# Down projections of three feed-forward blocks: weights stationary, or activations stationary with four pairs by seven products

## Chip, cores and metric

One Trainium2 chip, one core of it. The metric is the device time of one execution in microseconds; lower is better. A profiled execution gives a trace, from which the rows shown below are taken. TensorE is called PE, VectorE DVE, ScalarE ACT, GpSimd POOL; SP is the engine that issues the loads. Ldweights (PEld) puts a 128x128 tile, the stationary operand, into the PE array; a matmul then streams the columns of the moving operand past it.

## What is computed

Two decoder layers over 256 tokens of 1024 features, float32. Each layer is a half-weighted feed-forward block, attention, and another half-weighted feed-forward block:

```python
def swiglu(h, w_gate, w_up, w_down):
    return (jax.nn.silu(h @ w_gate) * (h @ w_up)) @ w_down

for layer in range(DEPTH):                      # 2
    h = h + 0.5 * swiglu(rmsnorm(h, ffn1_norm[layer]), ...)   # D_FF 2816
    hn = rmsnorm(h, mix_norm[layer])
    if layer == 0: h = h + mixer_a(hn, ...)     # own q, k, v
    else:          h = h + mixer_b(hn, ...)     # q from hn, shared k, v
    h = h + 0.5 * swiglu(rmsnorm(h, ffn2_norm[layer]), ...)
    if layer == 0: shared = shared_kv(h, kv_norm, kv_w, pos)
return rmsnorm(h, final_norm)
```

## The kernel before

The stream lives in `hT`, with features on partitions: eight blocks (`d`, or `k` where they are contracted) of 128 features by 256 tokens. The stages run in the order f10, mixer a, f20, f11, mixer b, f21; the name of a feed-forward block is `f`, which of its layer's two it is, and the layer.

*Products in two parts.* Every float32 operand is split into a high part (ACT copies it, rounded, into `wh`, or the first half of an `x`) and a low part (DVE subtracts the high one: `wl`, or the second half). A product is high x high + high x low + low x high. `products_t` (L190) holds weights stationary: `wh` against the 512 columns of an `x` block (high and low, 256 tokens each), then `wl` against the 256 high columns. `product` (L181) holds activations stationary, 128 tokens at a time, against three times 512 columns of weights.

*Feed-forward.* `ffn_blocks` (L354) makes the 22 blocks of 128 hidden features, two at a time, each with 8 + 8 matmuls for gate and for up; `close` joins the two halves of the accumulators, applies the norm's row, silu and the product, and splits the result. The three inner blocks then call `down_t` (L320): four passes over pairs of output blocks, each over all 22 hidden blocks with weights stationary; the sum goes straight into `hT` (L332), and `norm.block` (L218) makes the next norm's scaled block `x` and its square at once. Six of the eight output blocks are thus done before the last pass.

*The last one, f21,* calls `down_last` (L435) instead, with tokens on partitions. Its hidden blocks are taken in 11 pairs. Four of them (`FAST`: 2, 4, 6, 7) are computed as a 2x2 block product by seven block products in place of eight: `quarter_sums` (L342) forms sums of the activations during gate and up (the tiles `left`), `load` (L459) forms sums of the weights (DVE one addition, POOL two), `fast` (L476) issues the seven products into `m1`, `m5`, `m6`, `m7` and three of the four outputs `c11`, `c12`, `c21`, `c22`, and `collect` (L486) combines them after the last fast pair. Two pairs are held back to the end, so that the outputs close one by one.

*Norms.* `finish` (L234) turns the sum of squares (POOL adds, L232) into a column per token tile by a PE product, an addition on DVE and a power on POOL. A stage that follows can begin before it: the factor is applied when its first accumulators are evacuated.

*PSUM.* Eight banks: five for accumulators (`acc`) and three for transposes and small things (`trt`), each set taken in rotation.

*Mixers.* An `Agenda` (L257) puts small steps (rotation, transposes of queries and keys, scores, softmax, values) between projection products by planned delays. `projections` (L720) goes over segments of weights; for each, four blocks of token tile 0, four of tile 1, the other four of tile 0, of tile 1. `evacuate` (L698) follows a tile's last block.

The order of the instructions on each engine is made by a scheduler when the kernel is built; each engine then executes its own list strictly in order, waiting on semaphores. What is far apart in the code can stand close together there: the eight gains of the shared keys and values (`kx`, passed as `beside` to f11) stand within f20's down in the kernel before.

Of the kernel before, what the change touches and what calls it, by code (L numbers as in the profile page):

```python
# [15 lines left out]
P = 128  # L16
# [50 lines left out]
def trunk(ctx: ExitStack, tc: tile.TileContext, a: dict, out: bass.AP):  # L67
# [139 lines left out]
    def by_token(xs):  # L207

        return [[tuple(x[:, i, t * P:(t + 1) * P] for i in range(2)) for x in xs] for t in range(NT)]

    class Norm:

        def __init__(self, gi, name):
            self.gi, self.name, self.x, self.col, self.row = gi, name, [], None, None
# [103 lines left out]
    def down_t(name, w, blocks, norm):  # L320

        for p in range(KD // 2):
            acs = [acc(f"dn_{name}_{2 * p + b}") for b in range(2)]
            for k0 in range(0, KF, KD):
                k = min(KD, KF - k0)
                ws = unit(f"{name}_{p}_{k0}", k, S, [(None, rows(w, k0, k, p * S, S))])
                cut = [[tuple(v[:, b * P:(b + 1) * P] for v in pair) for pair in ws] for b in range(2)]
                products_t(acs, cut, blocks[k0:k0 + k], k0 == 0, k0 + k == KF)
            for b, ac in enumerate(acs):
                d = 2 * p + b  # L330
                for half in (ac[:, :S], ac[:, S:]):
                    nc.vector.scalar_tensor_tensor(hT[:, d, :], half, 0.5, hT[:, d, :], op0=ALU.mult, op1=ALU.add)  # L332
                norm.block(d)

# [19 lines left out]
    def ffn_blocks(name, wg, wu, norm, first=None, beside=(), sums=None):  # L354
# [42 lines left out]
        for f in range(0, KF, 2):  # L397
# [37 lines left out]
    def down_last(name, w, blocks, sums, h, weight, part, after, tail=2):  # L435
# [4 lines left out]
        c11, c12, c21, m1, m5 = [acc(f"dn_{name}_{n}") for n in ("11", "12", "21", "m1", "m5")]  # L440
        c22, m6, m7 = [trt(f"dn_{name}_{n}") for n in ("22", "m6", "m7")]
# [45 lines left out]

# [376 lines left out]
```

## Times and profile before

| what | value |
|---|---|
| three runs | 986.69, 986.85, 988.29 us; median 986.85 |
| profiled execution | 986.84 us, of which 985.1 is its span (first to last instruction) |
| granted PE clock | 0.999 |
| busy | PE 99%, weight loads 86%, DVE 76%, ACT 60%, POOL 22% |
| moved from memory | 173.99 MB at 178 GB/s |
| f_g, f_u matmuls (gate and up) | 688 of 512 columns and 688 of 256 columns each |
| dn_f matmuls (the three `down_t`) | 528 of 512 columns and 528 of 256 columns |

A row such as `L332 DVE ... gains_hT<-dn_f,gains_hT 128x256 ... x48 | 19.0, 417 | 23.1 <-PE dn_f L198` is a group: line, engine, operation, output and inputs, shape, count, then busy time in us, mean ns of one, idle time before it, and what ended the idle time. In the rows of the timeline the first two numbers are the start and the duration in us, and a bracket gives the idle time before and its releaser. Matmuls overlap, so the spacing of their starts says more than their durations. Numbers of tiles are left out in names: `wh_f_g` are the high parts of all gate weights, `x_n` the scaled blocks of all norms. The matmuls that a helper issues all carry the helper's line.

### The profile page before, as it was taken

The page shows a single profiled execution, that of the slowest core. Times are in us where ns is not written, and L with a number is a line of the kernel's source. Part 1 is how long each engine was busy: PE and PEld are TensorE (multiplying, and loading weights), DVE is VectorE, ACT ScalarE, POOL GpSimd, SP SyncE. Part 2 cuts the span into 40 slices and gives each one's busy share as a digit, 9 for nine tenths or more (in the row PEclk, how much of TensorE's full clock was granted, in tenths as well). Part 3 has the DMA queues.
Part 4 walks back from the last instruction along what each step waited for, and adds up shares of the span by engine and source line. Part 5 has one row for each costly group of instructions (what it writes and reads, how often), then busy time and mean ns, then how long its engine had stood idle before and what let it go on. Part 6 is the DMA issues. An engine that isn't in the chain of part 4 may idle for free.

```text
span 985.1 us, 15279 instructions
## 1 busy us (share of the span) xinstructions
PE 972.6 (99%) x5640; PEld 847.2 (86%) x5640; DVE 753.1 (76%) x1313; ACT 594.7 (60%) x1090; POOL 213.1 (22%) x220
## 2 busy tenths in 40 slices
PE   8999999999999999999999999999999999999997
PEld 5888888888889888888888888888888998888886
DVE  7987866677877788776668887657677778888996
ACT  7666654457776665654456556544577766666561
POOL 3211111122332211110112111111042422112461
PEclk9999999999999999999999999999999999999999
DMA  9876565655443556555655565665544255565351
GB/s 317 256 242 208 161 210 186 214 172 166 133 130 107 181 187 203 178 198 189 213 173 172 185 200 184 200 196 192 197 132 140 90 168 164 180 200 184 128 172 43
DMA packets 152251, 176.03 MB, mean 179 GB/s; under 512 B 3440, under 2 KB 140144, under 8 KB 152176
## 3 DMA queue, kind: packets, MB, share of 16 engines
q1 hardware_dynamic: 151328, 174.01, 55.1%
q8 instruction: 44, 0.72, 0.3%
q10 hardware_dynamic: 848, 1.05, 0.3%
q14 instruction: 31, 0.25, 0.1%
HBM read 173.99 MB, written 1.05 MB: 178 GB/s over the span
## 4 chain that ended last, share of the span: by engine, by line
PE 68%; ACT 2%; DVE 2%; issue 1%; POOL 0%; POOLq 0%; ACTq 0%; DVEq 0%
PE f_g L195 12%; PE f_u L195 12%; PE dn_f L195 8%; PE f_u L198 6%; PE f_g L198 6%; PE dn_f L198 4%; PE dn_f_d L184 1%; PE dn_f_d L186 1%; PE dn_f_d L188 1%; PE q_b L184 1%; PE kv_b L184 1%; PE q_b L188 1%; PE kv_b L188 1%; PE q_b L186 1%; PE kv_b L186 1%; PE ot_ao L546 1%
## 5 line engine op out<-in xcount | busy, mean ns | idle before, releaser
L195 PE MATMUL f_g<-x_n,wh_f_g 128*128 128x512 f32 x688 | 180.4, 394 | 0.0
L195 PE MATMUL f_u<-x_n,wh_f_u 128*128 128x512 f32 x688 | 177.3, 390 | 0.0
L371 POOL TENSOR_TENSOR j_f_u<-j_f_u,r_n 128x256 f32<-128x256 f32 x88 | 80.5, 917 | 376.2 <-DVE j_f_u L339 352.7
L195 PEld LDWEIGHTS f_u<-x_n,wh_f_u 128*128 128x128 f32 x688 | 129.2, 188 | 27.3
L195 PEld LDWEIGHTS f_g<-x_n,wh_f_g 128*128 128x128 f32 x688 | 124.0, 189 | 22.7
L195 PE MATMUL dn_f<-act_f,wh_f 128*128 128x512 f32 x528 | 126.5, 391 | 0.0
L159 DVE TENSOR_TENSOR wl_f_u<-raw_f_u,wh_f_u 128x1024 fp32r<-128x1024 f32 x86 | 118.5, 1380 | 2.9 <-ACT wh_f_u L158 2.8
L159 DVE TENSOR_TENSOR wl_f_g<-raw_f_g,wh_f_g 128x1024 fp32r<-128x1024 f32 x86 | 103.5, 1233 | 15.7 <-PE f_g L198 9.3
L195 PEld LDWEIGHTS dn_f<-act_f,wh_f 128*128 128x128 f32 x528 | 96.9, 188 | 18.6
L159 DVE TENSOR_TENSOR wl_f<-raw_f,wh_f 128x1024 fp32r<-128x1024 f32 x72 | 81.8, 1153 | 36.0 <-ACT wh_f L158 26.8
L198 PE MATMUL f_u<-x_n,wl_f_u 128*128 128x256 f32 x688 | 103.3, 283 | 0.0
L198 PE MATMUL f_g<-x_n,wl_f_g 128*128 128x256 f32 x688 | 102.7, 282 | 0.0
L198 PEld LDWEIGHTS f_g<-x_n,wl_f_g 128*128 128x128 f32 x688 | 96.4, 190 | 6.2
L158 ACT ACTIVATE wh_f<-raw_f 128x1024 fp32r<-128x1024 f32 x72 | 67.3, 978 | 49.5 <-PE dn_f L195 27.2
L158 ACT ACTIVATE wh_f_u<-raw_f_u 128x1024 fp32r<-128x1024 f32 x86 | 86.7, 1048 | 16.7 <-PE f_g L195 10.9
L158 ACT ACTIVATE wh_f_g<-raw_f_g 128x1024 fp32r<-128x1024 f32 x86 | 89.5, 1048 | 9.8 <-issue 6.0
L198 PEld LDWEIGHTS f_u<-x_n,wl_f_u 128*128 128x128 f32 x688 | 91.6, 192 | 0.0
L232 POOL TENSOR_TENSOR ss_n<-ss_n,sq_n 128x256 f32<-128x256 f32 x42 | 41.8, 996 | 221.6 <-ACT sq_n L231 220.7
L369 ACT ACTIVATE j_f_g<-j_f_g 128x256 f32<-128x256 f32 x88 | 36.7, 417 | 66.2 <-DVE j_f_g L368 65.8
L98 ACT ACTIVATE act_f<-j_f_g 128x256 fp32r<-128x256 f32 x80 | 33.0, 417 | 65.4 <-DVE j_f_g L379 65.3
L198 PEld LDWEIGHTS dn_f<-act_f,wl_f 128*128 128x128 f32 x528 | 68.1, 191 | 2.8
L198 PE MATMUL dn_f<-act_f,wl_f 128*128 128x256 f32 x528 | 69.0, 283 | 0.0
(553 smaller groups left out, 1795.8 us busy)
## 6 DMA issues: line engine op xcount, KB each, us to landing
raw_f_g<-in_ffn_w_gate_dram SPq DMA_DIRECT2D x43, 1024.0 KB, 5.4
raw_f_u<-in_ffn_w_up_dram SPq DMA_DIRECT2D x43, 1024.0 KB, 5.4
raw_f<-in_ffn_w_down_dram SPq DMA_DIRECT2D x24, 1024.0 KB, 5.2
raw_f_d<-in_ffn_w_down_dram SPq DMA_DIRECT2D x11, 1024.0 KB, 5.0
raw_f<-in_ffn_w_down_dram SPq DMA_DIRECT2D x12, 768.0 KB, 4.5
raw_qka<-in_a_w_qkv_dram SPq DMA_DIRECT2D x16, 512.0 KB, 4.3
raw_va<-in_a_w_qkv_dram SPq DMA_DIRECT2D x4, 1024.0 KB, 5.2
raw_ao<-in_a_w_o_dram SPq DMA_DIRECT2D x4, 1024.0 KB, 5.0
```

The lines of the kernel that those rows point to most:

```text
L98: nc.scalar.activation(hi, src, AF.Copy, scale=scale)
L158: nc.scalar.activation(wh, r, AF.Copy)
L159: nc.vector.tensor_sub(wl, r, wh.bitcast(F32))
L184: nc.tensor.matmul(ac, xh, wh, start=first, stop=False)
L186: nc.tensor.matmul(ac, xh, wl, start=False, stop=False)
L188: nc.tensor.matmul(ac, xl, wh, start=False, stop=last)
L195: nc.tensor.matmul(ac, wh, flat(x), start=first and i == 0, stop=False)
L198: nc.tensor.matmul(ac[:, :S], wl, x[:, 0, :], start=False, stop=last and i == len(ws) - 1)
L232: nc.gpsimd.tensor_tensor(self.ss, self.ss, sq, op=ALU.add)
L369: nc.scalar.activation(g, g, AF.Silu)
L371: nc.gpsimd.tensor_tensor(u, u, norm.row, op=ALU.mult)
L546: nc.tensor.matmul(ac, wl[:, d], hi, start=False, stop=k == KD - 1 and j == 1)
```

## The change

All four downs are now computed in the way of f21. The body of `down_last` becomes `quartered`, which returns a function `close` that finishes one output quarter (token tile `t`, feature half `c`). `down_last` uses it as before. The new `down` is used by f10, f20 and f11 in place of `down_t`:

- `collect` no longer adds to the stream; it returns four tiles (`co`), onto which the closed quarters are added (DVE, one operation each).
- The quarters close in the order (0,0), (1,0), (0,1), (1,1). `turn` transposes two feature blocks of both tiles into a `trt` bank (eight transposes for a half of 512 features, in two groups), adds them to `hT`, and norms the two blocks. The first half is turned ahead of the last block of quarter (0,1). The second half's two turns are put off (`norm.late`): a mixer's agenda takes them 1.5 and 2.0 after its start, a feed-forward block after its first contraction block.
- `x` is therefore looked up when it is used (`x[t](k)`), and in the mixers the column product of the norm and both evacuations of the first segment that needs it come after both token tiles.
- `left_sums` chooses where the quarter sums live. f10 and f20 have four homes, as f21 has; f11, in which the tiles of `kx` are in use, has three, and so three fast pairs (2, 4, 6) instead of four.
- Token tile 1's outputs `c21` and `c22` and the product `m6` now lie in the three transpose banks, `c11`, `c12`, `m1`, `m5`, `m7` in the accumulator banks.
- The gains `kx` now stand in f11's opening in ACT's and DVE's lists, not in f20's down.

```diff
@@ ffn_blocks, first two blocks
                             products_t([ac], [[(wh[:, cols], wl[:, cols])]], norm.x[k:k + 1], k == 0, k == KD - 1)
+                    while norm.late:
+                        norm.late.pop(0)()
@@
-    def ffn(name, layer, which, norm, after, first=None, beside=()):
+    def ffn(name, layer, which, norm, after, first=None, beside=(), homes=("kx4", "kx6", "qkh", "qkh")):
...
-        blocks = ffn_blocks(name, wg, wu, norm, first, beside)
+        sums = left_sums(homes)
+        blocks = ffn_blocks(name, wg, wu, norm, first, beside, sums)
...
-        down_t(name, wd, blocks, after)
+        down(f"{name}_d", wd, blocks, sums, after)
@@
-        c11, c12, c21, m1, m5 = [acc(f"dn_{name}_{n}") for n in ("11", "12", "21", "m1", "m5")]
-        c22, m6, m7 = [trt(f"dn_{name}_{n}") for n in ("22", "m6", "m7")]
+        c11, c12, m1, m5, m7 = [acc(f"dn_{name}_{n}") for n in ("11", "12", "m1", "m5", "m7")]
+        c21, m6, c22 = [trt(f"dn_{name}_{n}") for n in ("21", "m6", "22")]
@@
+        def close(t, c, cols=slice(0, 512), ac=None, between=None):
+            n = quarters[t][c][0] if ac is None else "end"
+            whole = quarters[t][c][1] if ac is None else ac
+            to = whole[:, :cols.stop - cols.start]
+            for j, (k, ws) in enumerate(held):
+                add(n, to, blocks[t][k], tuple(v[:, cols] for v in ws[c]), k == KF - 1)
+                if between is not None and j == len(held) - 2:
+                    between()
+            return whole
@@
+    def down(name, w, acts, sums, norm):
+        outs = []
+        close = quartered(name, w, acts, sums, 0.5, outs.extend)
+        def turn(c, half):
+            tr = trt(f"dt_{name}_{c}_{half}")
+            for i in range(2):
+                for t in range(NT):
+                    at = i * S + t * P
+                    nc.tensor.transpose(tr[:, at:at + P], outs[t][c][:, (2 * half + i) * P:(2 * half + i + 1) * P], ident)
+            d = 4 * c + 2 * half
+            h = hT[:, d:d + 2, :]
+            nc.vector.tensor_add(h, tr.rearrange("p (k s) -> p k s", s=S), h)
+            for i in range(2):
+                norm.block(d + i)
+        def turn_first():
+            for half in range(2):
+                turn(0, half)
+        for c in range(2):
+            for t in range(NT):
+                ac = close(t, c, between=turn_first if (t, c) == (0, 1) else None)
+                nc.vector.scalar_tensor_tensor(outs[t][c], ac, 0.5, outs[t][c], op0=ALU.mult, op1=ALU.add)
+        norm.late += [lambda half=half: turn(1, half) for half in range(2)]
@@ mixer
+        for norm in {id(norm): norm for norm, _, _ in segs}.values():
+            for i in range(len(norm.late)):
+                agenda.after(1.5 + 0.5 * i, lambda norm=norm: norm.late.pop(0)())
...
-                            product([acs[t]], *x[t][k], [w], k == 0, k == KD - 1)
+                            product([acs[t]], *x[t](k), [w], k == 0, k == KD - 1)
...
-                        if k0 + 4 == KD:
-                            if norm.col is None:
-                                norm.finish()
+                        if k0 + 4 == KD and norm.col is not None:
                             evacuate(i, t, norm.col[t], acs[t], parts)
+                if norm.col is None:
+                    norm.finish()
+                    for t in range(NT):
+                        evacuate(i, t, norm.col[t], acs[t], parts)
@@
-    ffn("f11", 1, 1, n3, n5, beside=[lambda k=k: kx.append(gain(k, 3, "kx", "kx")) for k in range(KD)])
+    ffn("f11", 1, 1, n3, n5, homes=("qkh", "qkh", "pT"), beside=[lambda k=k: kx.append(gain(k, 3, "kx", "kx")) for k in range(KD)])
```

More of the change, by code (lines that the diff above doesn't have):

```diff
@@ L317, in __getitem__ @@
             return self.parts[i]
[L320 to L333, printed above, removed]
     def joined(ac, name):
@@ L518, in down_last, with collected @@
+    def down_last(name, w, acts, sums, h, weight, part, after):
+        def collected(shared):
+            for t in range(NT):
+                for c in range(2):
+                    (nc.vector if t else nc.gpsimd).tensor_tensor(h[t][c], h[t][c], shared[t][c], op=ALU.add)
+        close = quartered(name, w, acts, sums, weight, collected)
         for t in range(NT):
             for c in range(2):
-                n, ac = quarters[t][c]
-                cut = 512 if (t, c) != (1, 1) else S
-                for k, ws in held:
-                    add(n, ac[:, :cut], blocks[t][k], tuple(v[:, :cut] for v in ws[c]), k == KF - 1)
+                n = 512 if (t, c) != (1, 1) else S
+                ac = close(t, c, slice(0, n))
```

46 lines of the change are left out of this document (24 added, 22 removed).

## Prediction

> **What bounds the kernel now.** I read the busy shares first, then what TensorE (PE) waits for, then single stages by windows.
>
> ```profile
> span 985.1 us, 15279 instructions
> PE 972.6 (99%) x5640; PEld 847.2 (86%) x5640; DVE 753.1 (76%) x1313; ACT 594.7 (60%) x1090; POOL 213.1 (22%) x220
> PEclk9999999999999999999999999999999999999999
> ...
> PE busy L118 <- DVE fill L115: 1.4, 1, 1.4
> PE f_g L195 <- ACT wh L173: 1.3, 2, 0.9
> PE po_b L637 <- DVE pT_b L94: 1.0, 1, 1.0
> ```
>
> PE is occupied 99% of the span at full clock, and its list of waits has six rows of 0.7 to 1.4 us, about 6 us in all. So time is won by issuing fewer PE columns and lost wherever PE begins to wait. The windows of the down stages (f10, f20, f11, f21 in the order of the program), and of f21's gate and up products, say what each costs (columns: length; PE, weight loads, DVE, ACT, POOL busy, each with its count; clock; DMA share; GB/s):
>
> ```profile
> 132.40:193.70 61.30, 61.30 (x355) 54.16 (x354) 38.46 (x51) 29.87 (x42) 7.40 (x6) 1.00 0.63 201
> 433.40:494.70 61.30, 61.30 (x355) 54.17 (x354) 40.84 (x56) 30.75 (x46) 7.71 (x6) 1.00 0.62 199
> 618.30:679.50 61.20, 61.20 (x354) 54.07 (x353) 38.46 (x49) 29.81 (x42) 7.76 (x6) 1.00 0.62 200
> 812.50:921.50 109.00, 109.00 (x639) 96.66 (x638) 90.70 (x158) 68.27 (x128) 22.05 (x22) 1.00 0.58 184
> 921.50:979.00 57.50, 57.46 (x266) 47.89 (x264) 50.23 (x54) 28.56 (x42) 28.60 (x13) 1.00 0.30 101
> ```
>
> The fifth row is the layout that the change gives to the other three: f21 already has act stationary and four pairs by seven products. PE never pauses there, nor in the stage before it (fourth row), where the quarter sums of the activations are formed. That is the best evidence in this case, because the copied work has been seen beside its own DVE, ACT and POOL load.
>
> **Part 1, the products.** Before, a down is 176 (block, output) pairs, each one 512-column and one 256-column matmul: 61.3/176 = 0.348 us. After, 7 ordinary pairs of 24 matmuls and 4 fast ones of 21 make 252 matmuls of 512 columns. f21 shows exactly that in 57.5 us, so 0.228 each; 12 of its matmuls are cut in two there, some 0.1 us. I take 57.4 for f10 and f20: **-3.9 us each**. f11 has homes for only three quarter sums, so 255 matmuls: 57.4 + 3 x 0.228 = 58.1, **-3.1 us**. Of the 3.9 about 2.7 is the four products left out (4 x 3 x 0.228) and 1.2 the orientation. SP issues 11 loads of 1024 KB per down for 12 smaller ones, the same 11 MB.
>
> **Part 2, the turns.** Each down adds 16 transposes of 128x128. The mixer's turn has the same form:
>
> ```profile
> 205.53 0.39 PE L188 MATMUL v_a<-wh_va,x_n 128*128 128x512 f32 x1
> 205.76 0.60 PE L692 MATMUL qt_a<-ident,rt_a 128*128 128x128 f32 x4
> 206.12 0.48 PE L184 MATMUL v_a<-wh_va,x_n 128*128 128x512 f32 x1
> 206.43 0.40 PE L186 MATMUL v_a<-wl_va,x_n 128*128 128x512 f32 x1
> ```
>
> Four take 0.36 us, and the next matmul takes 0.31 for 0.23, so two adjoining groups cost 0.36 + 0.36 + 0.08 = 0.8 us, and a down's two such places 1.6. **+4.8 us over three downs**, all on PE. Parts 1 and 2 together: -2.3, -2.3, -1.5, so **-6.1 us**.
>
> **Part 3, work that must stay hidden.** In gate and up, DVE gets the quarter sums and ACT their high halves; f21 hides the same. In the down, POOL adds eight half-blocks and DVE and ACT split seven pieces for four. One add was starved there:
>
> ```profile
> 934.30 11.38 POOL L468 TENSOR_TENSOR sum_f_d_6b<-sum_f_d_6ac,raw_f_d 128x512 f32<-128x512 f32 x1 [4.40 <-DVE sum_f_d_6ac L467]
> 948.61 1.56 DVE L455 TENSOR_TENSOR wl_f_d_6d<-sum_f_d_6d,wh_f_d_6d 128x512 fp32r<-128x512 f32 x1
> ```
>
> Pair 6 starts on PE after 138 matmuls, at 921.5 + 31.5 = 953.0, and first needs that last piece 15 matmuls later, at 956.4, while it is split by 950.2. The cover is 6 us; were it gone, PE would wait by the excess. I book zero.
>
> **Part 4, the hand-over to the next stage** is new, and its order shows in the built kernel. Let T be the end of the last product. Before, six of eight feature blocks were normed long before T. Now nothing of the stream is ready until both token tiles of a half are closed. The first turn (features 0 to 511) sits five products, 3.4 us, ahead of T; the second sits behind nine matmuls of the mixer (T+2.05), or behind the eight of f11's first block (T+1.4). Durations:
>
> ```profile
> 970.75 0.69 DVE L524 SCALAR_TENSOR_TENSOR h<-dn_f_d,h 128x512 f32<-128x512 f32 x1 [2.71 <-PE dn_f_d L188]
> 193.69 1.22 DVE L311 TENSOR_TENSOR wl_va<-raw_va,wh_va 128x1024 fp32r<-128x1024 f32 x1
> 922.40 2.31 DVE L455 TENSOR_TENSOR wl_f_d_2a<-raw_f_d,wh_f_d_2a 128x1024 fp32r<-128x1024 f32 x1
> L96 DVE SCALAR_TENSOR_TENSOR x_n<-gains_hT,x_n x48: 470/955/1049, 4.1 to 800.5; 128x256 fp32r<-128x256 f32 x48
> 195.28 0.51 ACT L98 ACTIVATE x_n<-gains_hT 128x256 fp32r<-128x256 f32 x1 [1.24 <-DVE gains_hT L332]
> 195.70 0.40 ACT L231 ACTIVATE sq_n<-gains_hT 128x256 f32<-128x256 f32 x1
> 192.03 2.01 ACT L309 ACTIVATE wh_va<-raw_va 128x1024 fp32r<-128x1024 f32 x2 [3.11 <-issue]
> 196.24 1.06 POOL L232 TENSOR_TENSOR ss_n<-ss_n,sq_n 128x256 f32<-128x256 f32 x1 [10.72 <-ACT sq_n L231]
> ```
>
> DVE, from T-3.6: two adds into hT (no row has the form; the 0.69 of the first row stands for it), low half of block 0, the closing sum of (tile 0, half 1), low halves 1 to 3, then the closing sum of (tile 1, half 1). ACT feeds it in steps of 0.4 to 0.5 and finishes high half 3 near T. A low half takes 0.47 alone and 0.96 beside a POOL add, and three POOL adds fall here. So block 3 is done at about T+1.5 and the last closing sum at T+2.2. The second turn waits for it: 0.8 us in f11, 0.15 in each mixer.
>
> *Mixer a, second half.* Behind the closing sum DVE has two weight splits (T+4.6), two adds (T+5.9), low half 4, a split of 1.22, then low halves 5 to 7. ACT has four weight copies until T+4.5. PE reaches block 4 at T + 24 x 0.228 + 0.8 + 0.15 = T+6.4 and wants low half 5 at T+7.5; DVE has it at T+8.0 to 8.4, or T+9.5 if the split takes the 2.31 of the third row. Between 0.4 and 2 us; I take 1.0, as most splits run near 1.22. The POOL sums end near T+10.5, before the column product at T+13.
>
> *f11, second half.* Blocks come 1.4 us apart, so low halves 4 to 7 are in time. But the eight shared-K/V gains, which f20's down used to hide, now stand on ACT in f11's opening, between a weight copy that waits for the last product of f11's first units and the copies that free the accumulators:
>
> ```profile
> 499.70 0.49 ACT L98 ACTIVATE x_kx<-gains_hT 128x256 fp32r<-128x256 f32 x1
> 506.00 0.50 PE L237 MATMUL col_n<-mean,ss_n 128*128 128x1 f32 x4
> 507.64 0.36 ACT L338 ACTIVATE j_f_g<-f_g 128x256 f32<-128x256 f32 x1
> 509.04 0.42 DVE L339 TENSOR_TENSOR j_f_g<-f_g,j_f_g 128x256 f32<-128x256 f32 x1
> 512.39 2.09 PE L195 MATMUL f_g<-x_n,wh_f_g 128*128 128x512 f32 x8
> ```
>
> Counted from the column product C: one copy to C+1.1, seven gains at 0.4 to C+3.9, two copies to C+5.9, the first accumulator copied and joined at C+6.8. PE wants its bank for the fourth block at C + (512.39 - 506.00) = C+6.4. A wait of 0.5 us, bounds 0 and 2.
>
> *Turn-in of queries.* The column product moved behind both token tiles, so both tiles' first turns now follow each other in each mixer:
>
> ```profile
> 202.65 0.71 POOL L241 TENSOR_TENSOR c_n<-v_n,expo 128x2 f32<-128x2 f32 x1 [2.99 <-DVE v_n L239]
> 203.39 0.69 ACT L703 ACTIVATE rt_a<-qk_a,c_n 128x512 f32<-128x512 f32 x1 [2.72 <-POOL c_n L241]
> 204.11 0.29 DVE L576 TENSOR_TENSOR ra_a<-rt_a,rot 128x128 f32<-128x128 f32 x1 [1.54 <-ACT rt_a L703]
> ```
>
> A split of 1.22 stands ahead of the small sum on DVE, then 0.71, two evacuations of 0.69 and eight rotations of 0.2 to 0.3: the second tile is ready near C+4.6, PE asks at C+4.2. **0.4 us in each mixer** (0 to 1).
>
> Waits together: mixer a 0.15 + 1.0 + 0.4, f11 0.8 + 0.5, mixer b 0.15 + 0.4, so **+3.4 us**, bounds 0 and 8. Where no wait comes, what hides it is the 5.5 to 6.4 us of PE work between a turn and the first use of its blocks.
>
> **The sum.** -6.1 + 3.4 = -2.7. The profiled execution took 986.84 us, 1.74 beyond its span, and the runs' median is 986.85; the same 1.74 stays. **984.1 us.**
>
> **Rivals.** (a) *All of Part 4 hides*, as f21's stage hides all of its own: 986.85 - 6.1 = 980.7. For it: the order was built with these chains in sight. Against it: the closing sum ends 0.8 behind PE's arrival in f11 by rows alone.
> (b) *The f11 opening costs more*: gains that f20's down hid become a wait, the join of the first accumulators late by the upper bound of 2 us, and DVE, held by a split behind the waiting copy, late with the row of norms too, another 0.5: 984.1 + 2.0 = 986.1, no change that can be told.
> (c) *Slower: DVE and POOL collide at the hand-over.* Each turn puts seven POOL adds among DVE's low halves and weight splits. If every one is slowed (eight low halves by 0.49, two splits by 1.09), DVE's chain is 6.1 us longer; 1.5 us of slack taken off, mixer a and f11 wait 4.6 more each and mixer b 1 more: 984.1 + 10.2 = 994.3, and with two thirds of it 990.9, which I take as its time. It decides from 4.7 us on (988.8). Against it: many splits of 1.2 us ran beside POOL adds as well.
> (d) *The products don't come denser*, PE waiting for the pieces of fast pairs: 1 us in each of the 11 gives 984.1 + 11 = 995. f21's row speaks against it.
>
> The Trainium skill, page "SBUF — State Buffer", section "Who interferes with whom", says that VectorE with two SBUF inputs and a GpSimd operation lock each other out for a whole instruction, and that issue order decides who waits. By it a low half would wait out a whole add, 1.06 us in place of my 0.49, and a turn with eight of them would be 4.6 us later still: an estimate that makes (c) the case. The trace agrees that they collide (0.47 against 0.96; the add of 11.38), but shows partial delays rather than a whole add for every operation.
>
> **Chances.** Sum as worked out (982.2 to 986) 0.52; (a) 0.20; (b) 0.14; (c) 0.11; (d) 0.03. The range 980.4 to 988.0 holds the first three and leaves out 14 in 100. Less than 0.2% (2 us) can't be told from no change here. Faster than 984.9: (a) and most of the first, 0.64; within 0.2%: the rest of the first and (b), 0.22; slower: 0.14.
>
> **What would show it.** The windows of the three downs: 57.4 + 0.8 us with PE full (Part 1 and first turn), f11's 58.1 + 0.8. Two groups of four transposes at 0.36 each. PE's waits: dt on DVE's closing sum of about 0.8 in f11 and under 0.3 in the mixers; qk_a's third matmul of blocks 5 to 7 on x_n; f_g of f11's fourth block on the join; qt on the rotations. If PE's list shows none of these, (a) holds; if gate and up stages or the fast pairs show waits, f21 was a bad guide and the sum falls.

## The result, and the profile after

The changed kernel took 984.54 us (median of 7 runs, 984.32 to 984.83) beside 986.91 us for the kernel before in the same comparison: a ratio of 0.9972, with a 95% interval of 0.996 to 0.9983. It is faster by 2.4 us; the prediction said 984.1. The profiled execution's span fell from 985.1 to 982.6 us. The head of the page after, and its list of what PE waited for:

```profile
span 982.6 us, 14865 instructions
PE 968.3 (99%) x5391; PEld 832.8 (85%) x5391; DVE 813.0 (83%) x1383; ACT 613.8 (62%) x1131; POOL 289.6 (29%) x242
...
PE qt_a L741 <- DVE rt_a L625: 1.7, 1, 1.7
PE busy L118 <- DVE fill L115: 1.4, 1, 1.4
PE qt_b L741 <- DVE rt_b L625: 1.0, 1, 1.0
```

PE executes 249 matmuls fewer. VectorE is busy 60 us more and GpSimd 77 us more, and yet the list has only two rows that are new: the query turns of the two mixers. The windows of the downs of f10, f11 and f21 (the first two up to their last product, so with their first turn; the second figure is PE's busy time):

```profile
132.40:190.50 58.10, 58.10 (x263) 48.20 (x262) 50.61 (x56) 34.08 (x50) 27.12 (x12) 1.00 0.61 211
...
616.10:674.90 58.80, 58.80 (x266) 48.74 (x265) 47.57 (x52) 32.40 (x47) 22.30 (x10) 1.00 0.60 207
918.90:976.40 57.50, 57.50 (x266) 47.94 (x264) 50.27 (x53) 28.52 (x42) 28.64 (x13) 1.00 0.29 101
```

PE is busy in all of 58.10 and 58.80 us: the new downs run as f21's always did, with one turn on top. To see where time went I read, in PE's timeline, when each stage's first product starts, and took the length of each stage (us):

| stage | before | after | difference |
|---|---|---|---|
| f10 down | 61.25 | 58.04 | -3.21 |
| mixer a (from its first product to f20's) | 116.20 | 119.57 | +3.37 |
| f20 down | 61.25 | 58.07 | -3.18 |
| f11 opening (to the column product) | 11.31 | 12.17 | +0.86 |
| f11, rest of gate and up | 112.26 | 112.25 | 0 |
| f11 down | 61.25 | 58.76 | -2.49 |
| mixer b | 116.66 | 118.78 | +2.12 |
| gate and up of f20 / f21 | 123.57 / 125.33 | 123.57 / 125.32 | 0 |

The stages add up to -2.5, the change of the span. Three downs give 8.9 us, and the stage behind each takes some back: 0.86 in f11, 2.1 in mixer b, 3.4 in mixer a. About 0.87 of each is the second turn itself. The rest is late starts: 2.5 us in mixer a and 1.25 in mixer b, of which PE's idle time in the timeline shows 1.7 and 1.1 (a product that waits also starts its follower some 0.1 us late, and very short waits leave no gap). Mixer a's hand-over in the timeline of after, first PE and ACT, then DVE, then POOL:

```profile
202.76 0.50 PE L238 MATMUL col_n<-mean,ss_n 128*128 128x1 f32 x4
...
208.46 1.23 PE L741 MATMUL qt_a<-ident,rt_a 128*128 128x128 f32 x8 [1.65 <-DVE rt_a L625]
206.53 1.27 ACT L752 ACTIVATE rt_a<-qk_a,c_n 128x512 f32<-128x512 f32 x2 [2.51 <-POOL c_n L242]
196.90 2.73 DVE L96 SCALAR_TENSOR_TENSOR x_n<-gains_hT,x_n 128x256 fp32r<-128x256 f32 x3
199.55 1.75 DVE L312 TENSOR_TENSOR wl_va<-raw_va,wh_va 128x1024 fp32r<-128x1024 f32 x1
201.23 3.48 DVE L312 TENSOR_TENSOR wl_qka<-raw_qka,wh_qka 128x1024 fp32r<-128x1024 f32 x3
204.64 0.15 DVE L240 TENSOR_SCALAR v_n<-col_n 128x2 f32<-128x2 f32 x1
204.71 1.21 DVE L312 TENSOR_TENSOR wl_qka<-raw_qka,wh_qka 128x1024 fp32r<-128x1024 f32 x1
195.78 4.45 POOL L233 TENSOR_TENSOR ss_n<-ss_n,sq_n 128x256 f32<-128x256 f32 x4 [3.86 <-ACT sq_n L232]
204.87 1.62 POOL L242 TENSOR_TENSOR c_n<-v_n,expo 128x2 f32<-128x2 f32 x1 [4.64 <-DVE v_n L240]
```

The column product is issued at 202.76, but the small sum that reads it (v_n) starts only at 204.64: DVE has no gap from 196.90 on, and the sum comes only behind the third split of the row above it, 1.88 us after the column product. Then the power (c_n) takes 1.62 us where it took 0.71 before. ACT gets both tiles' evacuations at 206.53, and PE, which had nothing else in its order, stands still for 1.65 us.

### The profile page after: what moved, and what is told of

Read it like the earlier page. It is cut to its first block, busy times and chain, and to the rows that moved or that the text cites. A ratio compares the mean times of both kernels' runs of the same rounds, so it can differ in the third digit from the quotient of the medians.

```text
span 982.6 us, 14865 instructions
## 1 busy us (share of the span) xinstructions
PE 968.3 (99%) x5391; PEld 832.8 (85%) x5391; DVE 813.0 (83%) x1383; ACT 613.8 (62%) x1131; POOL 289.6 (29%) x242
## 3 DMA queue, kind: packets, MB, share of 16 engines
q10 hardware_dynamic: 848, 1.05, 0.3%
HBM read 173.99 MB, written 1.05 MB: 178 GB/s over the span
## 4 chain that ended last, share of the span: by engine, by line
PE 68%; ACT 2%; DVE 2%; issue 1%; POOL 0%; POOLq 0%; ACTq 0%; DVEq 0%
PE f_g L195 12%; PE f_u L195 12%; PE f_u L198 6%; PE f_g L198 6%; PE dn_f_d L188 5%; PE dn_f_d L186 5%; PE dn_f_d L184 5%; PE dn_f_d_m L188 1%; PE dn_f_d_m L186 1%; PE dn_f_d_m L184 1%; PE q_b L184 1%; PE q_b L188 1%; PE q_b L186 1%; PE ot_ao L592 1%; PE ot_ao L590 1%; PE kv_b L184 1%
## 5 line engine op out<-in xcount | busy, mean ns | idle before, releaser
L357 POOL TENSOR_TENSOR j_f_u<-j_f_u,r_n 128x256 f32<-128x256 f32 x88 | 92.3, 1051 | 360.9 <-DVE j_f_u L325 338.1
L159 DVE TENSOR_TENSOR wl_f_u<-raw_f_u,wh_f_u 128x1024 fp32r<-128x1024 f32 x86 | 113.1, 1317 | 2.7 <-ACT wh_f_u L158 2.7
L233 POOL TENSOR_TENSOR ss_n<-ss_n,sq_n 128x256 f32<-128x256 f32 x42 | 38.4, 914 | 148.3 <-ACT sq_n L232 146.3
L98 ACT ACTIVATE act_f<-j_f_g 128x256 fp32r<-128x256 f32 x58 | 23.9, 418 | 56.6 <-DVE j_f_g L365 56.6
L365 DVE TENSOR_TENSOR j_f_g<-j_f_g,j_f_u 128x256 f32<-128x256 f32 x58 | 27.9, 487 | 30.1 <-POOL j_f_u L357 30.1
L473 POOL TENSOR_TENSOR sum_f_d_6b<-sum_f_d_6ac,raw_f_d 128x512 f32<-128x512 f32 x4 | 45.5, 11374 | 17.6 <-DVE sum_f_d_6ac L472 13.2
L325 DVE TENSOR_TENSOR j_f_g<-f_g,j_f_g 128x256 f32<-128x256 f32 x88 | 36.7, 417 | 11.9 <-ACT j_f_g L324 11.9
L664 POOL TENSOR_SCALAR sm_b<-sm_b,ls_b 128x128 f32<-128x128 f32 (+1 forms) x32 | 29.8, 949 | 44.0 <-DVE ls_b L662 34.3
L664 POOL TENSOR_SCALAR sm_a<-sm_a,ls_a 128x128 f32<-128x128 f32 (+1 forms) x32 | 28.0, 890 | 50.0 <-DVE ls_a L662 32.8
L324 ACT ACTIVATE j_f_u<-f_u 128x256 f32<-128x256 f32 x88 | 33.0, 375 | 14.7 <-PE row_n L250 13.7
```

Source lines behind the costliest of these rows:

```text
L159: nc.vector.tensor_sub(wl, r, wh.bitcast(F32))
L233: nc.gpsimd.tensor_tensor(self.ss, self.ss, sq, op=ALU.add)
L325: nc.vector.tensor_add(s, ac[:, :S], s)
L357: nc.gpsimd.tensor_tensor(u, u, norm.row, op=ALU.mult)
L473: nc.gpsimd.tensor_tensor(b[:, 0], ac[:, 0], raw[:, 3], op=ALU.add)
L664: nc.gpsimd.tensor_scalar(sm[:, seg], sm[:, seg], ls[:, t:t + 1], None, op0=ALU.mult)
```

## Experiments

All runs are changes of the changed kernel (984.54). Each was compared with the kernel before on its own chip, which took 986.9 to 987.3 us there. The stage lengths that moved, from the same reading of PE's timeline; the gate and up stages stayed within 0.06 us and are left out:

| run | f10 down | mixer a | f20 down | f11 down | mixer b | median, us |
|---|---|---|---|---|---|---|
| after | 58.04 | 119.57 | 58.07 | 58.76 | 118.78 | 984.54 |
| early column | 58.04 | 119.66 | 58.07 | 58.76 | 117.54 | 983.45 |
| later turn | 58.04 | 117.58 | 58.07 | 58.76 | 119.61 | 983.91 |
| one fast pair | 60.08 | 119.63 | 60.11 | 60.11 | 118.82 | 990.17 |
| banks | 58.04 | 119.62 | 58.08 | 58.75 | 118.88 | 984.58 |
| no late squares | 58.04 | 118.43 | 58.07 | 58.75 | 118.79 | 983.33 |
| copy behind the power | 58.04 | 118.92 | 58.07 | 58.75 | 118.15 | 983.02 |
| best of both | 58.04 | 117.63 | 58.07 | 58.76 | 117.56 | 981.76 |
| early column, later turn | 58.04 | 117.86 | 58.08 | 58.72 | 117.50 | 981.50 |
| and a fourth pair in f11 | 58.04 | 117.83 | 58.07 | 58.08 | 117.56 | 981.02 |
| and a fifth pair, early | 60.88 | 117.81 | 59.90 | 58.08 | 117.55 | 985.94 |
| and a fifth pair, late | 62.02 | 117.37 | 59.44 | 58.08 | 117.52 | 986.01 |

The first product of f10's down starts between 132.23 and 133.08 in these executions, which is a wait in the program's opening and no effect of the edits; the stage lengths are free of it.

### What the products are worth: one fast pair, and the banks

```diff
-    def ffn(..., homes=("kx4", "kx6", "qkh", "qkh")):
+    def ffn(..., homes=("kx4",)):
-    ffn("f11", ..., homes=("qkh", "qkh", "pT"), ...)
+    ffn("f11", ..., homes=("qkh",), ...)
```

> The changed kernel with one pair by seven products in each of the three converted downs in place of four: 9, 9 and 8 groups fewer are saved (8 groups of 3 matmuls of 512 columns in all come back, 0.228 us each). Theory: each product left out is worth 3 x 0.228 = 0.68 us and nothing else in these stages binds, so 8 x 0.68 = 5.5 us more than the changed kernel, 990.0, which is slower than the kernel before: orientation alone does not pay for the two turns and the waits behind them. Rival: the fast pairs' sums on GpSimd and splits on VectorE disturb the hand-over, so that fewer of them also take waits away: then it is less than 5.5 us slower, 987 to 988.5.

(The first figures of that text should be 3, 3 and 2 products; its sum of eight is right.) 990.17 us, a ratio to before of 1.003 (1.0019 to 1.004): 5.6 us more than after, and slower than before. The downs grew by 2.04, 2.04 and 1.35 us, which is 0.68 for each of the eight products that came back, and mixer a stayed at 119.6. So the theory holds: the fast pairs carry the gain, and fewer of them take no wait away. Orientation with one fast pair loses against its turns and waits. The rows also give an estimate for orientation alone: f10's down with one fast pair, less its turn of 0.87 and with the 0.68 of that pair added, is 59.9 us, 1.36 below the 61.25 of before, and the down's two turns cost 1.74.

```diff
-        c11, c12, m1, m5, m7 = [acc(...) for n in ("11", "12", "m1", "m5", "m7")]
-        c21, m6, c22 = [trt(...) for n in ("21", "m6", "22")]
+        c11, c12, c21, m1, m5 = [acc(...) for n in ("11", "12", "21", "m1", "m5")]
+        m6, m7, c22 = [trt(...) for n in ("m6", "m7", "22")]
```

> The changed kernel with the bank of the second token tile's first half exchanged: its accumulator goes back among the accumulator banks and one of the fast pairs' combination banks goes to the turning banks instead. Theory: where the second tile's accumulator stands decides only which bank comes free first at the hand-over, and all of those waits are under 0.4 us: within 0.5 us of 984.5. Rival: the bank's place frees an accumulator bank early enough for the next stage's first products, and without it PE waits for the closing sums at each of the three hand-overs, some 0.5 to 1 us each: 986 to 987.5.

984.58 us, ratio 0.997 (0.9959 to 0.998), and every stage within 0.1 us of after. Which of these banks holds the second tile's first half makes no measurable difference; only this one exchange was tried.

### Where the mixers' waits come from

The first pair of runs moves the column product into the loop over the token tiles, or asks for the turn later in the segment that finishes the norm. The early column:

```diff
-                        if k0 + 4 == KD and norm.col is not None:
+                        if k0 + 4 == KD:
+                            if norm.col is None:
+                                norm.finish()
                             evacuate(i, t, norm.col[t], acs[t], parts)
-                if norm.col is None:
-                    norm.finish()
-                    for t in range(NT):
-                        evacuate(i, t, norm.col[t], acs[t], parts)
```

> The changed kernel, but in both mixers the norm's column product follows the first token tile's last block again and each token tile is evacuated and turned by itself, as before the change. Theory: the 1.7 us (mixer a) and 1.0 us (mixer b) that PE waits for the query turns come from the column's place behind both tiles: the small sum then stands behind weight splits on VectorE, the GpSimd power runs beside a split, and both tiles' turns follow each other. Then both waits vanish and the time is about 2.7 us less, 981.9. In mixer a the sum of squares ends about when the earlier column product wants it, so 0 to 0.5 us may come back as a wait of the column product. Rival 1: only the small sum's place behind the splits matters less than the stream itself being late, so a wait of the same length moves to the column product or to the scores: the time stays at 984.5. Rival 2: the wait is that of the two tiles turned together alone; then it vanishes too, and this run cannot tell it from the theory (the next one can).

The later turn:

```diff
-                    agenda.after(3.2, turn_in, g, t)
+                    agenda.after(wait, turn_in, g, t)
-                        evacuate(i, t, norm.col[t], acs[t], parts)
+                        evacuate(i, t, norm.col[t], acs[t], parts, 5.8)
```

> The changed kernel, but the query turn of each token tile in the two mixers is put 12 matmuls (2.7 us) further behind its evacuation, with the column product left where the change has it. Theory: PE waits only because the turned queries are asked for too early for the chain of sum, power and rotations; asked 2.7 us later both waits (1.7 and 1.0 us) go, and scores follow 2.7 us later with other products in between: about 2.7 us less, 981.8. Rival: the scores and the softmax behind them are then late and PE runs out of products; a wait of 1 to 3 us appears at the scores or at the attention's values, and the time stays within 1 us of 984.5.

983.45 and 983.91 us, ratios 0.9961 (0.9947 to 0.9974) and 0.9967 (0.9955 to 0.998). Each theory was right in one mixer. The early column gave mixer b back its 1.24 us and mixer a nothing; the later turn gave mixer a 1.99 us, but mixer b ended 0.83 longer. The timeline of the run with the early column shows why mixer a was not helped (PE, DVE, POOL):

```profile
200.21 0.60 PE L238 MATMUL col_n<-mean,ss_n 128*128 128x1 f32 x4
...
205.94 0.63 PE L741 MATMUL qt_a<-ident,rt_a 128*128 128x128 f32 x4 [1.59 <-ACT wh_qka L310]
202.30 0.15 DVE L240 TENSOR_SCALAR v_n<-col_n 128x2 f32<-128x2 f32 x1
202.53 1.62 POOL L242 TENSOR_TENSOR c_n<-v_n,expo 128x2 f32<-128x2 f32 x1 [2.37 <-DVE v_n L240]
```

The column came 2.55 us earlier, and so did PE's request of the turn, which follows it at a fixed distance. The chain between them is as long as before: the small sum again waited 2 us for DVE, the power again took 1.62, and PE again stood 1.6 us. (The name after the arrow is what the profile infers; the turn reads the rotated rows, which DVE ended at 205.8.) Here the two tiles are turned one by one and PE waits as long, so the rival of the two turns together falls for mixer a. In mixer b DVE is waiting when the column comes, and the power has no split beside it (such rows follow below). There the small sum, the power and the two tiles' turns all change at once, and this run does not separate them.

With the later turn, mixer b's query turn no longer waits, but two of its later scores wait for DVE's turned weights of the softmax:

```profile
721.80 0.32 PE L643 MATMUL s_b<-qkh_b 64*128 64x128 f32 x1 [0.29 <-DVE pT_b L94]
730.92 0.32 PE L643 MATMUL s_b<-qkh_b 64*128 64x128 f32 x1 [0.29 <-DVE pT_b L94]
```

These two waits are 0.6 us, less than the 1.05 that went. More is lost in the scores themselves. Their stationary tiles fill 64 of PE's 128 rows (64*128 in the row), and they come in groups of twelve that run two at a time: a group takes 0.88 us from start to start. With the later turn the third group is parted by k products and the first of these waits: six scores at 719.89 take 0.88 us, and the other six at 721.80 take 0.88 again. The fourth group, whose second half waits, takes 1.61. All scores of mixer b take 9.10 us for 7.50 in after, and the k products 12.18 for 11.63.

The second pair joins what worked. In "best of both" mixer a has the later turn and mixer b the early column:

```diff
+                        if k0 + 4 == KD and norm.col is None and name == "b":
+                            norm.finish()
...
+                        evacuate(i, t, norm.col[t], acs[t], parts, 5.8)
```

In the other the column is early in both, and mixer a's first turns are asked 1.8 us later:

```diff
+                            late = name == "a" and i == 0
+                            evacuate(i, t, norm.col[t], acs[t], parts, 5.0 if late else 3.2)
```

> The changed kernel with the query turns of mixer a asked 2.7 us later (the column product stays behind both token tiles) and, in mixer b, the column product back behind the first token tile. Theory: the two mixers need different mends, because at mixer a's hand-over VectorE is behind with its work and at mixer b's it is not; each mend keeps what it brought alone (2.0 us at mixer a by the distance of the same program points, 1.2 us at mixer b): 3.2 us less than the changed kernel's 984.5, 981.3. Rival: the gain at mixer a is given back further on, as the one at mixer b was when its turns were asked later: 983.3.

> The changed kernel with the column product behind the first token tile in both mixers and, in mixer a alone, the query turns of the opening segment asked 1.8 us later. Theory: with the earlier column PE still waited 1.6 us in mixer a, as the small sum stands behind 2 us of VectorE's backlog and the power beside a split; a request 1.8 us later meets the turned tile ready, so the 1.6 us goes and mixer b keeps its 1.2: 981.7, and no wait for the rotations in the list. Rival: the chain of the scores is what binds in mixer a, and the wait reappears there: 983.3.

981.76 and 981.50 us, ratios 0.9942 (0.993 to 0.9954) and 0.9939 (0.9926 to 0.9953); the two do not differ clearly. The gains add up, near the 981.3 and 981.7 expected, and no query turn is left in PE's list of waits.

### Why VectorE is late in mixer a

```diff
-                nc.gpsimd.tensor_tensor(self.ss, self.ss, sq, op=ALU.add)
+                if k < 4 or self.name not in ("n1", "n3", "n5"):
+                    nc.gpsimd.tensor_tensor(self.ss, self.ss, sq, op=ALU.add)
```

> The changed kernel without GpSimd's adds of the squares of the last four feature blocks in the three norms behind a converted down; it leaves these blocks out of the mean of squares. Theory: at mixer a's hand-over VectorE is late because its low halves (0.9 us each) and a split (1.75 us) run beside these adds. Without them a low half takes about 0.47 and the split 1.2, VectorE gains 1.5 to 2.3 us, the small low-half waits (0.3 to 0.5 us) and most of the 1.7 us at the query turn go: 982.5 to 983.3. At mixer b the adds end long before the column product, so the 1.0 us there stays. Rival: the backlog is the order of the work (splits ahead of the small sum) and not the collision: then the 1.7 us stays within 0.4 and the time within 0.6 us of 984.5.

983.33 us, ratio 0.9957 (0.9945 to 0.997); mixer a is 1.14 us shorter and mixer b unchanged. As this kernel leaves out part of the sum of squares, it is a measurement and not a version to use. Its timeline (PE, DVE, POOL), to be read against the same rows of after:

```profile
202.40 0.50 PE L239 MATMUL col_n<-mean,ss_n 128*128 128x1 f32 x4
...
207.46 1.23 PE L742 MATMUL qt_a<-ident,rt_a 128*128 128x128 f32 x8 [1.01 <-DVE rt_a L626]
197.03 1.27 DVE L96 SCALAR_TENSOR_TENSOR x_n<-gains_hT,x_n 128x256 fp32r<-128x256 f32 x3
198.22 1.22 DVE L313 TENSOR_TENSOR wl_va<-raw_va,wh_va 128x1024 fp32r<-128x1024 f32 x1
203.70 1.79 POOL L243 TENSOR_TENSOR c_n<-v_n,expo 128x2 f32<-128x2 f32 x1 [11.66 <-DVE v_n L241]
```

Three low halves take 1.27 us where they took 2.73 beside GpSimd's adds, and the split 1.22 for 1.75: 2 us of DVE's lateness was the collision of the two engines. About half of it reached PE: the small waits for low halves go (the column product is reached 0.49 us sooner after the stage's start), and the wait at the turn falls from 1.65 to 1.01. It does not vanish, since the small sum still stands behind a split and the power still takes 1.79; ahead of that split DVE now idles 0.62 us for ACT's copy of the weight, and so loses part of what it gained. The rival, that only the order counts, falls for these 1.1 us and stays open for the other 1.0.

The power itself shows a clean pattern over the program. Rows of after: POOL's powers in f20's opening, in f11's opening and in mixer b, and what DVE ran beside the last two.

```profile
322.11 0.72 POOL L242 TENSOR_TENSOR c_n<-v_n,expo 128x2 f32<-128x2 f32 x1 [7.51 <-DVE v_n L240]
...
506.82 0.88 POOL L242 TENSOR_TENSOR c_n<-v_n,expo 128x2 f32<-128x2 f32 x1 [6.22 <-DVE v_n L240]
...
698.85 1.78 POOL L242 TENSOR_TENSOR c_n<-v_n,expo 128x2 f32<-128x2 f32 x1 [14.27 <-DVE v_n L240]
506.66 0.47 DVE L96 SCALAR_TENSOR_TENSOR x_kx<-gains_hT,x_kx 128x256 fp32r<-128x256 f32 x1
698.84 1.23 DVE L312 TENSOR_TENSOR wl_kb<-raw_kb,wh_kb 128x1024 fp32r<-128x1024 f32 x1
```

Alone it takes 0.72, beside a short low half 0.88, beside a split 1.62 or 1.78. In each of the last three it ends 0.56 to 0.57 us after the end of the DVE operation beside it. All 13 kept traces show the same: 0.70 to 0.72 with nothing of DVE beside it, 0.87 to 0.88, 1.62, and 1.78 to 1.79. With the early column and the later turn, mixer b's power is alone again; there DVE had waited for the column (the bracket):

```profile
693.52 0.16 DVE L240 TENSOR_SCALAR v_n<-col_n 128x2 f32<-128x2 f32 x1 [0.69 <-PE col_n L238]
693.77 0.70 POOL L242 TENSOR_TENSOR c_n<-v_n,expo 128x2 f32<-128x2 f32 x1 [10.98 <-DVE v_n L240]
```

The Trainium skill, page "SBUF — State Buffer", sections "Who interferes with whom" and "Summary: rules for kernel authors", says that when a VectorE instruction has two SBUF inputs and a GpSimd operation reads SBUF, the one that issues second waits until the first is done. By it, as an estimate with 0.72 for the power alone, the three would take what is left of the DVE operation and 0.72: 1.05 + 0.72 = 1.77, 1.22 + 0.72 = 1.94 and 0.31 + 0.72 = 1.03. The trace nearly agrees: 1.62, 1.78 and 0.88 are each about 0.15 shorter.

I tried to take the split away from the power:

```diff
+            if self.name in ("n1", "n5"):
+                held = sp.tile([P, NT], F32, tag="rmsv", name=f"h_{self.name}")
+                nc.vector.tensor_copy(held, r)
+                r = held
             self.col = [r[:, t:t + 1] for t in range(NT)]
```

> The changed kernel with a tiny VectorE copy of the norm's column right behind the small sum in the two converted mixers; the copy waits for GpSimd's power, so that VectorE runs no split while the power runs. Theory: the power takes 1.6 to 1.8 us only because a split of 1.2 us runs beside it; alone it takes about 0.7, as before the change, so the turned queries come 0.8 to 0.9 us earlier: the waits at the query turns fall from 1.7 to about 0.8 and from 1.0 to about 0.1, and the time is about 1.8 us less, 982.8. Rival: the power's time is its own in this place (the gap on GpSimd ahead of it), it stays at 1.6 us or more, the copy only holds up the split, and the time is 984.5 to 985.5.

983.02 us, ratio 0.9965 (0.9951 to 0.9978), nearly the time expected, for another reason. Its timeline (DVE, POOL, PE):

```profile
204.51 1.21 DVE L316 TENSOR_TENSOR wl_qka<-raw_qka,wh_qka 128x1024 fp32r<-128x1024 f32 x1
206.32 0.17 DVE L245 COPY h_n<-c_n 128x2 f32<-128x2 f32 x1 [0.60 <-POOL c_n L242]
204.67 1.62 POOL L242 TENSOR_TENSOR c_n<-v_n,expo 128x2 f32<-128x2 f32 x1 [4.64 <-DVE v_n L240]
208.28 0.63 PE L745 MATMUL qt_a<-ident,rt_a 128*128 128x128 f32 x4 [0.97 <-DVE rt_a L629]
```

The order of work put the split ahead of the copy again, so the power still ran beside it. What changed is PE's order: it has 18 matmuls between column product and turn for 15, in both mixers, so the turn is asked three matmuls (0.68 us) later and its waits fall by just that, from 1.65 to 0.97 and from 1.04 to 0.38. So the run says nothing on the power; it confirms that the moment of the request sets the wait. What the power alone would bring was not run. Mixer b's rows allow an estimate. In after its column product starts at 697.50, and the small sum stands behind one split:

```profile
698.61 0.15 DVE L240 TENSOR_SCALAR v_n<-col_n 128x2 f32<-128x2 f32 x1
```

That is 1.11 us later; in the run with the early column it is 0.54. The power takes 1.78 and 0.70, and the first tile is rotated 4.95 and 3.12 us after the column product. So of the 1.83 us won, 1.08 is the power, as much as the whole wait of 1.04 at that turn: an estimate, since no run changed the power by itself.

### How far the fast pairs go

On top of "early column, later turn", the place of the final gain, loaded later, was used for one more set of quarter sums: first in f11, then in f10 and f20 too, as pair 1 or as pair 8. The fourth pair in f11:

```diff
-    gfin = const.tile([P, D], F32, name="gfin")
...
+    gfin = [xp.tile([P, 512], F32, tag=f"gf{c}", name=f"gfin_{c}") for c in range(2)]
...
-    ffn("f11", ..., homes=("qkh", "qkh", "pT"), ...)
+    ffn("f11", ..., homes=("qkh", "qkh", "pT", "gf0"), ...)
```

The fifth pair, here as pair 1; the late one has FAST + (8,) in its place:

```diff
-    def ffn(..., homes=("kx4", "kx6", "qkh", "qkh")):
+    def ffn(..., homes=("kx4", "kx6", "qkh", "qkh", "gf0")):
-        for i, home in zip(FAST, homes):
+        for i, home in zip(FAST if len(homes) < 5 else (1,) + FAST, homes):
```

> The kernel with the earlier column product and mixer a's later turn (981.5), and a fourth pair by seven products in f11's down; its quarter sums use the place of the final gain, which is loaded after f11. Theory: one more product saved, 3 x 0.228 = 0.68 us: 980.8. Rival: f11's down has no room on VectorE for another fast pair, or the late load of the final gain holds up f21's weights: 981.5 to 983.

> As the run with the fourth pair in f11, and a fifth pair by seven products in f10 and f20 each (pair 1 of the eleven). Theory: each is worth 0.68 us as long as PE still has no wait in the downs, where VectorE is busy 50.6 of 58.1 us: 2 x 0.68 less, 979.5. Rival: VectorE becomes the bound: it has some 3.5 us more to do per pair by seven products (three splits and a two-row sum) in a stage 0.7 us shorter, and the pieces of pairs 1 and 2 come late, PE waits 1 us or more in each of the two downs: 981 to 983.

> As the run with the fifth pair, but the fifth is pair 8 in place of pair 1, so that it stands late in the down, away from the end of gate and up. Theory (the place): with pair 1 VectorE had to finish the last activations and make the pieces of pairs 1 and 2 at once, while later it has room; then each fifth pair is worth its 0.68 us and the time is 979.7. Rival (the stage as a whole): three pairs in a row, 6, 7 and 8, need more of VectorE than a stage of 57.4 us leaves beside 50.6 us of work, the pieces of pairs 7 and 8 come late and so does the hand-over: 982 to 986.

The fourth pair in f11 is worth what it saves: f11's down is 0.64 us shorter than in "early column, later turn" and the time 981.02 us, ratio 0.9938 (0.9926 to 0.9951). This is the fastest version measured. A fifth pair in f10 and f20 costs 5 us in both places tried: 985.94 and 986.01 us, ratios 0.9993 (0.9985 to 1.0002) and 0.9994 (0.9985 to 1.0003). With the early one, PE's list of waits, and f10's window (DVE is the fourth figure: 55.40 us busy):

```profile
PE dn_f_d_m L184 <- DVE wl_f_d_2a L458: 2.4, 2, 1.2
...
PE dn_f_d L184 <- DVE wl_f_d_1d L458: 1.4, 2, 0.7
132.40:193.00 60.60, 58.28 (x259) 46.99 (x258) 55.40 (x59) 36.04 (x52) 26.15 (x13) 1.00 0.60 208
```

VectorE goes from 50.6 us of work in f10's down to 55.4, in a stage that should last 57.4, and PE now waits for its splits at pairs 1 and 2. Counted by its starts, PE is late there by 3.4 us in f10; less the 0.68 saved, that is nearly all of the 2.8 that this down grew. Placed late, the pair moves the wait to the end. There DVE has no gap from the splits of pair 7 to the closing sums, and the first turn comes late. The run's waits, its windows around f10's end, PE's timeline at the two sides of the turn and at f20's turn, and two rows of DVE ahead of f10's turn (the clock is the third figure from the right in a window):

```profile
PE dt_f_d L539 <- DVE co_f_d_a L553: 3.4, 2, 2.0
...
187.00:188.00 1.00, 0.00 (x0) 0.00 (x0) 1.00 (x2) 0.00 (x0) 0.00 (x0) 1.00 1.09 367
...
188.50:191.50 3.00, 2.78 (x11) 2.46 (x11) 1.84 (x4) 0.99 (x3) 0.00 (x0) 0.50 1.02 326
...
188.25 0.38 PE L539 MATMUL dt_f_d<-ident,co_f_d_a 128*128 128x128 f32 x1 [2.03 <-DVE co_f_d_a L553]
...
190.83 0.63 PE L184 MATMUL dn_f_d<-wl_f_d_10b,act_f 128*128 128x512 f32 x1
191.25 0.63 PE L186 MATMUL dn_f_d<-wh_f_d_10b,act_f 128*128 128x512 f32 x1
...
490.03 0.33 PE L539 MATMUL dt_f_d<-ident,co_f_d_a 128*128 128x128 f32 x1 [1.34 <-DVE co_f_d_a L553]
...
180.58 2.35 DVE L310 TENSOR_TENSOR wl_qka<-raw_qka,wh_qka 128x1024 fp32r<-128x1024 f32 x2
...
187.52 0.68 DVE L553 SCALAR_TENSOR_TENSOR co_f_d_a<-dn_f_d,co_f_d_a 128x512 f32<-128x512 f32 x1
```

The theory of the place falls. The rival, the stage as a whole, fits, but another is open: four splits of the next stage's weights (two in the row at 180.58, two more behind it, 4.8 us by their durations) stand in DVE's list among the sums that close the down. They stand so in after too, where DVE still waits 1.9 us for PE behind them; here nothing is left. Whether the fifth pair would pay with these splits behind the closing sums was not tried.

The loss has a second part here: after a pause of 2.03 us the granted clock was 0.50 from about 188.5 to 191.7, and a matmul took 0.42 us from start to start. f10's down lost 4.0 us against the run with four pairs. Counted by PE's starts, 2.7 us of it is at the turn and 0.5 at a late split before it; the stretch at the slower clock takes 1.5 us more than the same instructions with the early pair, and 0.68 is saved. In f20 the pause was 1.34 us, the clock stayed at 1.00, and the loss was 1.37.

## Why the prediction was right

**Part 1 (products), right, a little small.** Predicted -3.9, -3.9 and -3.1, with 0.8 for the first turn in the same stage: -3.1, -3.1, -2.3. Measured -3.21, -3.18, -2.49. f21 was a good guide, and the run with one fast pair gives 0.68 us a product, the 3 x 0.228 of the sum.

**Part 2 (turns), right.** Each place costs about 0.87 us for 0.8; in f11's opening, where the second turn meets no wait, the difference is 12.17 - 11.31 = 0.86.

**Part 3 (hidden work), right, and now with a bound.** Booked at zero, and PE has no wait in any down. The add that took 11.38 us in f21 takes 11.4 on average in the four downs of after, as its group shows:

```profile
L473 POOL TENSOR_TENSOR sum_f_d_6b<-sum_f_d_6ac,raw_f_d 128x512 f32<-128x512 f32 x4 | 45.5, 11374 | 17.6 <-DVE sum_f_d_6ac L472 13.2
```

But the cover is thin: one more fast pair in f10 and f20 makes PE wait for VectorE and costs 5 us. Rival (d), PE waiting for the pieces, did not come at four pairs and came in kind at five.

**Part 4 (hand-over): the total was right by luck, its places were not.** Predicted 3.4 us, measured 3.75: mixer a 2.50 for 1.55, f11 0 for 1.3, mixer b 1.25 for 0.55. Four terms were mis-sized.

- *The second turn's wait on the last closing sum* (0.8 in f11, 0.15 in each mixer) did not come. In f11 the closing sum ended 1.44 us after the next stage's first product started (491.66, the prediction's T), not 2.2, just as PE came to the turn. And *the shared gains in f11's opening* (0.5) cost nothing: ACT needs 2.89 us for the seven, and the prediction had a weight copy ahead of them wait for PE. It did not wait, and the seven were done at 503.36, ahead of the column product (503.83); the first join ended at 509.68, before PE wanted its bank at 510.22. From the timeline of after:

```profile
492.42 0.68 DVE L555 SCALAR_TENSOR_TENSOR co_f_d_d<-dn_f_d,co_f_d_d 128x512 f32<-128x512 f32 x1
493.07 0.27 PE L541 MATMUL dt_f_d<-ident,co_f_d_b 128*128 128x128 f32 x1
500.47 2.89 ACT L98 ACTIVATE x_kx<-gains_hT 128x256 fp32r<-128x256 f32 x7
509.27 0.41 DVE L325 TENSOR_TENSOR j_f_g<-f_g,j_f_g 128x256 f32<-128x256 f32 x1
510.22 1.63 PE L195 MATMUL f_g<-x_n,wh_f_g 128*128 128x512 f32 x6
```

- *Mixer a's low halves* (1.0) cost 0.39: the stage reaches its first V product 12.67 us after its start for 11.41, and 0.87 of the 1.26 is the turn.
- *The turn-in of queries* (0.4 in each mixer, bounds 0 to 1) is where the time went: 2.1 us in mixer a, above its bound, and 1.25 in mixer b. The step put one split of 1.22 ahead of the small sum and took the power at 0.71. In mixer a the small sum started 1.88 us after the column product for 1.11 in mixer b, since DVE came late, in part from the collisions that were counted only for the low halves; and in both mixers the power ran beside a split, at 1.62 and 1.78. It was priced from a row in which it had POOL and DVE to itself.

So the low halves and f11 were charged too much and the query turn too little, and the two nearly cancelled. The total came within 0.5 us on Parts 1 to 3, which were sound, and on luck in Part 4. What Part 4 had right is the kind of loss: PE meets short chains on DVE and POOL at the hand-over, and the query turns are where the trace shows it. Rival (b), a costly opening of f11, did not come. Rival (c) named the right mechanism for mixer a, a DVE and POOL collision, and made it far too big: the low halves did slow from 0.42 to 0.91, but removing the late adds is worth 1.2 us, where its case had 6.8. Rival (a), all hidden, would have been 980.7; the best version, with one pair more, came to 981.02.

## What to carry to other kernels

A stage that already runs in the wanted form prices the copied products to one or two tenths of a microsecond a stage; the risk lies in the hand-over. Where results now close only at a stage's end, list every instruction that stands ahead of each small operation on the chain to the next stage, and price that operation beside the neighbour that it will have, not alone. Before saving more work on the bound engine, look at how full the helper already is: at 50.6 of 58 us a further 0.68 us saved in each of two downs cost 5 in all.

## What the runs showed of the hardware that was not expected

A tiny GpSimd power (128x2) took 0.72 us alone and 1.62 to 1.78 beside a VectorE split of 1.2 us with two inputs in SBUF. Three low halves took 1.27 us without GpSimd's adds and 2.73 beside them, so each was held up by 0.49, which is part of an add of 1.1 and not the whole.

In one execution a pause of PE of 2.03 us was followed by some 3.2 us at a granted clock of 0.50; pauses of 1.65 and 1.34 us were not. The Trainium skill, page "TensorE: Matmul & The Clock Gate", section "Part 1: The HAM clock gate", gives half rate as the state after at least one idle window, full rate after a busy one, and a window of about 3.4 us that runs free of the program. The depth agrees with the trace and the length nearly does; the pause was shorter than such a window, so this trace does not bear out that a whole idle window is needed. What set off the drop was not tested.
